# Gate and up of 20 FFN tiles as seven half-products in the place of eight

## The chip, the cores and the metric

The kernel runs on one core of one Trainium2 chip. The metric is the device time of one execution in microseconds (us); lower is better. The clock of TensorE (PE) was granted in full in every stretch of the profile.

## What is computed

One decoder layer of 1056 tokens (1024 of a prompt, 32 of eight short sequences) and 1024 features, all in fp32. The change touches the second FFN only:

```python
def swiglu_ffn(x, w_gate, w_up, w_down):
    return (jax.nn.silu(x @ w_gate) * (x @ w_up)) @ w_down
...
x = x + 0.5 * swiglu_ffn(rms_norm(x, ffn1[0]), ffn1[1], ffn1[2], ffn1[3])
y, h_last, new_conv, new_k, new_v = token_mixer(rms_norm(x, mix[0]), pos, h0, conv_buf, ...)
x = x + y
x = x + 0.5 * swiglu_ffn(rms_norm(x, ffn2[0]), ffn2[1], ffn2[2], ffn2[3])
```

`w_gate` and `w_up` are 1024 x 2816, `w_down` is 2816 x 1024.

## The kernel before

Features lie on the 128 partitions and tokens on the columns. The tokens are two halves: g=0 with 512 columns, g=1 with 544, which is two chunks of 272 (`CB`). The second half runs behind the first, and its FFN2 (`ffn(3, 1, ...)`) is the last piece of the program, with nothing beside it.

Every fp32 matrix product is three passes with the narrower type fp32r. Weights and activations are split into a high part (`whi`, `xh`) and the rest (`wlo`, `xl`), and PE adds whi.xh + whi.xl + wlo.xh (`mm3`, `mm3w`, lines 380 to 392). In g=1 each pass is two matmuls of 272 columns, one for each chunk, into two PSUM banks.

Weights come in units of 128 x 1024 fp32 (512 KB). SP loads a unit into one of two `raw` buffers, ACT writes `whi` (line 359), DVE writes `wlo` (line 361); three slots (`wslots`) hold split units. A gate or an up unit of an FFN tile f (128 of the 2816 columns) is 8 k-blocks x 3 passes x 2 chunks = 48 matmuls in g=1. So an ordinary tile of g=1 (`gu`) is 96 matmuls. A down unit is 48 as well. There are 22 tiles and 22 down units in g=1; down units stand in groups (two behind tile 3, then four behind tiles 6, 10, 14 and 18, four at the end).

In a tile of g=1 ACT takes silu of the gate out of PSUM (line 529), DVE multiplies it with the up product from PSUM (line 543), ACT and DVE split the result into `ha` for the down matmuls (lines 547, 549), and DVE adds each down product to x (`evd`, line 556). `prenorm` (lines 488 to 506) makes xh and xl for a stage; for the last stage it runs while PE works on the last down units of g=0.

No order is written by hand. The program is built by a planner in Python (`Sched`): each step is a generator that asks for an engine with a planned duration (`Req`), and the step that can start first is emitted next. The engines then run their queues in order, and wait on semaphores. A planned duration decides only the order.

Of the kernel before, what the change touches and what calls it, by code (L numbers as in the profile page):

```python
# [206 lines left out]
def layer(ctx: ExitStack, tc, t):  # L208
# [8 lines left out]
    NBIG, NPF, NH, NRM, NRAW, NW, NMX, NLW = 23, 3, 5, 6, 2, 3, 4, 1  # L217
# [33 lines left out]
    big, pff, hs, rms, banks = Pool(range(16, NBIG)), Pool(range(NBIG, NBIG + NPF)), Pool(range(NH)), Pool(range(NRM)), Banks()  # L251
# [88 lines left out]

    def loader():
        for n in range(2 * FIRST, len(order)):
            tk = yield Req("Q", 0.6, raws.soon(), when=raws.has(), lat=4.0)
            raw_of[n] = raws.get()[0]
            load_piece(n, 0)
            done(("raw", n, 0), tk)

    def splitter():
        for ns in [range(FIRST)] + [[n] for n in range(FIRST, len(order))]:
            for i, s in enumerate(pieces_of(ns[0])):  # L350
# [45 lines left out]
    def group(n, j, g, srcs, deps):  # L396
# [114 lines left out]
    def ffn(st, g, st2, u0, mode, rslot=None):
# [48 lines left out]
        def gu(f):  # L560
# [15 lines left out]
            if f == NF - 1:  # L576
                xfree(st2, g)

        xv = {m: ("x", st, g, m) for m in range(KD)}

        def down(gi, m0, mp):
            grp = GROUPS[gi]
            n = unit()
# [32 lines left out]
        for fn, k in steps:  # L616
# [784 lines left out]
    for g in range(2):  # L1401
# [3 lines left out]
        sc.spawn(prenorm(3, "g2", g), 2)  # L1405
# [133 lines left out]
```

## Time and profile before

| | |
|---|---|
| time, median of 3 runs | 1860.28 us (1860.11 to 1860.49) |
| the profiled execution: its own time | 1858.6 us |
| its span, first to last instruction | 1856.5 us |
| PE busy | 1850.5 us (100%), 11634 matmuls |
| DVE busy | 1064.3 us (57%) |
| ACT busy | 790.4 us (43%) |
| POOL busy | 12.3 us (1%) |
| DMA | 187.97 MB, mean 101 GB/s |

A matmul's own duration in the profile is longer than its step to the next one, since matmuls are pipelined; the distance between two starts is what one costs.

### The profile page before, as it was taken

How to read it: one execution, taken by the hardware profiler on the slowest of the kernel's cores; microseconds unless marked ns; L12 is line 12 of the kernel's file. 1: busy time of each engine (PE TensorE's matmuls, PEld its weight loads, DVE VectorE, ACT ScalarE, POOL GpSimd, SP SyncE). 2: the span in 40 equal slices, each digit the busy share in tenths (PEclk: the TensorE clock that was granted, in tenths of full speed). 3: DMA queues.
4: the chain of work that ended last, by engine and by line, in shares of the span. 5: the costliest groups of instructions: out<-in, count | busy, mean ns of one | idle time of the engine just before them, and what ended most of it. 6: DMA issues, size and time to landing. Idle time of an engine off the chain costs nothing.

```text
span 1856.5 us, 27927 instructions
## 1 busy us (share of the span) xinstructions
PE 1850.5 (100%) x11634; PEld 1691.5 (91%) x11634; DVE 1064.3 (57%) x1638; ACT 790.4 (43%) x1176; POOL 12.3 (1%) x39
## 2 busy tenths in 40 slices
PE   9999999999999999999999999999999999999999
PEld 7888888899999999999988988888898999999999
DVE  6774444466665777546576676865654543233333
ACT  6442222344746476424356566654533322222221
POOL 0000000000000000000000000000000000000000
PEclk9999999999999999999999999999999999999999
DMA  5432323242222322322242322232332422222222
GB/s 172 142 102 92 102 91 124 91 148 94 93 97 82 94 69 88 126 91 91 92 156 89 116 91 82 82 98 96 115 115 91 136 84 88 91 87 86 91 91 83
DMA packets 60253, 187.97 MB, mean 101 GB/s; under 512 B 7376, under 2 KB 9936, under 8 KB 60112
## 3 DMA queue, kind: packets, MB, share of 16 engines
q1 hardware_dynamic: 59984, 186.09, 30.3%
q8 instruction: 91, 1.49, 0.3%
q14 instruction: 34, 0.28, 0.0%
q10 hardware_dynamic: 144, 0.10, 0.0%
HBM read 174.58 MB, written 9.90 MB: 99 GB/s over the span
## 4 chain that ended last, share of the span: by engine, by line
PE 99%; DVE 0%; DMA 0%; ACT 0%; SPq 0%; issue 0%; ACTq 0%
PE ps L391 25%; PE ps L392 25%; PE ps L381 15%; PE ps L382 15%; PE ps L383 15%; PE ps L1060 1%; PE ps L795 0%; PE ps L1023 0%; PE ps L1022 0%; PE ps L1079 0%; PE ps L1078 0%; PE ps L911 0%; PE ps L317 0%; DMA fa<-x 0%; PE ps L1186 0%; DVE fa L556 0%
## 5 line engine op out<-in xcount | busy, mean ns | idle before, releaser
L359 ACT ACTIVATE whi<-raw 128x1024 fp32r<-128x1024 f32 (+1 forms) x312 | 325.3, 1043 | 686.7 <-issue 249.1
L361 DVE TENSOR_TENSOR wlo<-raw,whi 128x1024 fp32r<-128x1024 f32 (+1 forms) x312 | 375.4, 1203 | 194.0 <-ACT whi L359 188.1
L381 PE MATMUL ps<-xh,whi 128*128 128x512 f32 x880 | 345.2, 392 | 0.4 <-ACT xh L474 0.4
L383 PE MATMUL ps<-xh,wlo 128*128 128x512 f32 x880 | 342.9, 390 | 0.0
L382 PE MATMUL ps<-xl,whi 128*128 128x512 f32 x880 | 342.8, 390 | 0.1
L391 PE MATMUL ps<-xl,whi 128*128 128x272 f32 x880 | 254.4, 289 | 0.0
L392 PE MATMUL ps<-xh,wlo 128*128 128x272 f32 x880 | 254.2, 289 | 0.0
L391 PE MATMUL ps<-xh,whi 128*128 128x272 f32 x880 | 254.1, 289 | 0.0
L392 PE MATMUL ps<-xh,whi 128*128 128x272 f32 x880 | 253.5, 288 | 0.0
L391 PE MATMUL ps<-xh,wlo 128*128 128x272 f32 x880 | 253.4, 288 | 0.0
L392 PE MATMUL ps<-xl,whi 128*128 128x272 f32 x880 | 251.9, 286 | 0.0
L556 DVE SCALAR_TENSOR_TENSOR fa<-ps,fa 128x512 f32<-128x512 f32 (+1 forms) x192 | 135.6, 707 | 167.8 <-PE ps L392 100.7
L383 PEld LDWEIGHTS ps<-xh,wlo 128*128 128x128 f32 x880 | 165.2, 188 | 35.0
L381 PEld LDWEIGHTS ps<-xh,whi 128*128 128x128 f32 x880 | 165.4, 188 | 33.8 <-ACT xh L474 1.1
L382 PEld LDWEIGHTS ps<-xl,whi 128*128 128x128 f32 x880 | 165.3, 188 | 33.0 <-DVE xl L476 0.5
L391 PE MATMUL ps<-ha,whi 128*128 128x272 f32 x704 | 190.3, 289 | 0.0
L392 PE MATMUL ps<-ha,whi 128*128 128x272 f32 x704 | 189.8, 287 | 0.0
L391 PEld LDWEIGHTS ps<-xh,whi 128*128 128x128 f32 x880 | 165.8, 188 | 1.6
L392 PEld LDWEIGHTS ps<-xh,whi 128*128 128x128 f32 x880 | 165.4, 188 | 1.5
L391 PEld LDWEIGHTS ps<-xh,wlo 128*128 128x128 f32 x880 | 166.3, 189 | 0.0
L392 PEld LDWEIGHTS ps<-xh,wlo 128*128 128x128 f32 x880 | 166.0, 189 | 0.0
L392 PEld LDWEIGHTS ps<-xl,whi 128*128 128x128 f32 x880 | 165.9, 189 | 0.0
(238 smaller groups left out, 2723.0 us busy)
## 6 DMA issues: line engine op xcount, KB each, us to landing
raw<-w SPq DMA_DIRECT2D x304, 512.0 KB, 3.3
fa<-x SPq DMA_DIRECT2D x8, 272.0 KB, 3.8
xs<-fa SPq DMA_DIRECT2D x8, 272.0 KB, 4.9
fa<-xs SPq DMA_DIRECT2D x8, 272.0 KB, 2.9
y<-fa SPq DMA_DIRECT2D x8, 272.0 KB, 2.0
fa<-x SPq DMA_DIRECT2D x8, 256.0 KB, 4.4
xs<-fa SPq DMA_DIRECT2D x8, 256.0 KB, 4.2
fa<-xs SPq DMA_DIRECT2D x8, 256.0 KB, 3.4
```

Source lines behind the costliest of these rows:

```text
L359: S.activation(hi, raw, AF.Copy)
L361: V.tensor_tensor(lo, raw, f32(hi), OP.subtract)
L381: PE.matmul(p, wh, ah, start=first, stop=False)
L382: PE.matmul(p, wh, al, start=False, stop=False)
L383: PE.matmul(p, wl, ah, start=False, stop=last)
L391: PE.matmul(ps[:, b, :CB], w, a[:, c0], start=s, stop=e)
L392: PE.matmul(ps[:, b + 1, :CB], w, a[:, c1], start=s, stop=e)
L556: V.scalar_tensor_tensor(x, P_(b, g), fac, x, op0=OP.mult, op1=OP.add)
L1060: PE.transpose(ps[:, bk, j * 128:(j + 1) * 128], P[j // 2][:, j % 2, hf * 128:(hf + 1) * 128], ident)
```

## The change

In g=1 the gate and up products of tiles 2 to 21 are computed by Strassen's scheme in Winograd's form. Let x1 and x2 be features 0 to 511 and 512 to 1023, a and b the two chunks, G1, G2, U1, U2 the halves (512 rows) of the tile's gate and up weights. The eight half-products of a tile become seven, each 4 k-blocks x 3 passes = 12 matmuls of 272 columns, on sums of weights and sums of activations:

- weights: s1 = U1+U2, s2 = s1-G1, s3 = G2-s2, s4 = G1-U1, four POOL additions of 128 x 512 for every tile (`sums`);
- activations: T1 = x1b-x1a, T2 = x2b-T1, T3 = x2b-x1b, T4 = x2a-T2, 16 POOL subtractions of 128 x 272 once (`xsums`), then split by ACT and DVE (`small`); T1 to T3 go where xh and xl of g=0 were, T4 over x1b once the two ordinary tiles are through;
- products in PE's order: P1 = x1a.G1, P5 = T1.s1, P6 = T2.s2, P3 = x2b.s3, P7 = T3.s4, P2 = x2a.G2, P4 = T4.U2.

P1, P6, P7 and P4 are added up in one bank. ACT copies this bank into SBUF behind P1, P6 and P7 (`copy_of`), and the next of them waits for the copy. P5 and P3 share a second bank, copied behind P5; P2 has a third. `ev7` makes the tile's result out of the three banks and the four copies.

Gate and up weights of such a tile are loaded as four pieces of 128 x 512 into general buffers (`fa`) and split as seven pieces of 128 x 512, two in a slot. Three more `fa` buffers and a fourth one for tile results are added; the buffers of x of g=0 are given back when its output is stored. The first two of the last four down units run abreast.

```diff
-    NBIG, NPF, NH, NRM, NRAW, NW, NMX, NLW = 23, 3, 5, 6, 2, 3, 4, 1
+    NBIG, NPF, NH, NRM, NRAW, NW, NMX, NLW = 26, 4, 5, 6, 2, 3, 4, 1
...
     def loader():
-        for n in range(2 * FIRST, len(order)):
+        n = 2 * FIRST - 1
+        while n + 1 < len(order):
+            n += 1
+            if n in pairs:
+                tk = yield Req("Q", 1.0, tok["xt",], big.soon(4), when=lambda: big.n() >= (4 if summing[0] else 8) and waiting[0] < 2, lat=4.0)
+                waiting[0] += 1
+                raw_of[n] = [big.get()[0] for _ in range(4)]
+                for i, r in enumerate(raw_of[n]):
+                    SP.dma_start(F(r, 0), t["w"][order[n + i // 2], :, i % 2 * 512:i % 2 * 512 + 512])
+                done(("raw", n, 0), tk)
+                n += 1
+                continue
...
+    def sums(n, ss):
+
+        g1, g2, u1, u2 = (F(i, 0) for i in raw_of[n])
+        a, b, c, d = (F(i, 0) for i in ss)
+        for i, (o, x, y, op) in enumerate(((a, u1, u2, OP.add), (b, a, g1, OP.subtract), (c, g2, b, OP.subtract), (d, g1, u1, OP.subtract))):
+            tk = yield Req("G", 1.3, tok["raw", n, 0])
+            G.tensor_tensor(o, x, y, op)
+            done(("sum", n, i), tk)
...
+    def split_pair(n):
+
+        yield Req("G", 0.0, tok["raw", n, 0], big.soon(4), when=big.has(4))
+        ss = [big.get()[0] for _ in range(4)]
+        summing[0] += 1
+        sc.spawn(sums(n, ss), 1)
+        g1, g2, u1, u2 = raw_of[n]
+        wplace[n] = []
+        for i, (src, dep) in enumerate(((g1, 0), (ss[0], 1), (ss[1], 1), (ss[2], 1), (ss[3], 1), (g2, 0), (u2, 0))):
+            dep = tok[("sum", n, i - 1) if dep else ("raw", n, 0)]
+            if i % 2 == 0:
+                tk = yield Req("A", 0.55, dep, wslots.soon(), when=wslots.has())
+                wplace[n].append(wslots.get()[0])
+            else:
+                tk = yield Req("A", 0.55, dep)
+            c = slice(i % 2 * 512, i % 2 * 512 + 512)
+            hi, lo = whi_t[:, wplace[n][-1], c], wlo_t[:, wplace[n][-1], c]
+            S.activation(hi, F(src, 0), AF.Copy)
+            tk = yield Req("D", 0.6, tk)
+            V.tensor_tensor(lo, F(src, 0), f32(hi), OP.subtract)
+            done(("w", n, i), tk)
+        waiting[0] -= 1
+        summing[0] -= 1
+        big.put(Tok(max(tk.t, tok["sum", n, 3].t)), *raw_of[n], *ss)
+
...
-                               when=lambda: banks.has(1 + g)() and main_out[0] + g < MAINCAP)
+                               when=lambda: banks.has(1 + g)() and main_out[0] + g < (8 if tok['plain', 3, 1].t else MAINCAP))
...
+    def xsums(ys, k, tk):
+        (y1a, y1b), (y2a, y2b) = ((ys[m][:, :CB], ys[m][:, CB:]) for m in (k, k + 4))
+
+        for o, x, y in ((y1a, y1b, y1a), (y1b, y2b, y1b), (y2b, y2b, y1a), (y2a, y2a, y2b)):
+            tk = yield Req("G", 0.85, tk)
+            G.tensor_tensor(o, x, y, OP.subtract)
+        done(("xsum", k), tk)
...
+    def prenorm_pairs(st, name, g):
...
+        big.put(Tok(0.0), *range(NBIG - 3, NBIG))
+        yield Req("A", 0.0, big.soon(9), when=big.has(9))
+        tmp = [big.get()[0] for _ in range(9)]
+        out, *ys = (F(i, g) for i in tmp)
+        done(("xt",), Tok(0.0))
...
+        for m in range(KD + 1):
+            if m < KD:
+                tk = yield Req("D", dD(g))
+                V.scalar_tensor_tensor(ys[m], xap(m, g), col(name, m), out, op0=OP.mult, op1=OP.mult)
+                tkn = yield Req("A", dA(g), tk)
+                S.activation(xh[g][:, m], ys[m], AF.Copy)
+            if m:
+                m -= 1
+                tkd = yield Req("D", dD(g), tka)
+                V.tensor_tensor(xl[g][:, m], ys[m], f32(xh[g][:, m]), OP.subtract)
+                done(("xs", st, g, m), tkd)
+            tka = tkn
+            if m >= 4:
+                sc.spawn(xsums(ys, m - 4, tkd), 1)
+        big.put(tkd, tmp[0])
...
+        for i in range(4):
+            if i == 3:
+                yield Req("A", 0.0, tok["plain", st, g])
+            for k in range(4):
+                (y1a, y1b), (y2a, y2b) = ((ys[m][:, :CB], ys[m][:, CB:]) for m in (k, k + 4))
+                yield from small((y1a, y2b, y1b, y2a)[i], i, k, tok["xsum", k])
+                if i > 1:
+                    big.put(tok["xt", i, k], tmp[1 + k + 4 * (i == 3)])
...
+        def copy_of(b, to, tk, name, f):
+            tk = yield Req("A", 0.33, tk)
+            S.activation(to, ps[:, b, :CB], AF.Copy)
+            done((name, f), tk)
...
+        def ev7(f, bs, a, c):
...
+            tk = yield Req("D", dh, tok["P3", f], tok["mV", f])
+            V.tensor_tensor(a[:, z1], q, a[:, z1], OP.add)
...
+            tk = yield Req("D", dh, tok["P2", f])
+            V.tensor_tensor(a[:, z0], p, a[:, z0], OP.add)
...
+            tks = yield Req("A", dA(g), tk, sets=(S_SET,))
+            S.activation(a, a, AF.Silu)
+            yield Req("D", dh, tok["mW", f])
+            V.tensor_tensor(c[:, z1], c[:, z0], c[:, z1], OP.add)
+            yield Req("D", dh, tks)
+            V.tensor_tensor(c[:, z1], c[:, z1], a[:, z1], OP.mult)
...
+            tk = yield Req("D", dh, tok["P4", f])
+            V.tensor_tensor(c[:, z0], v, a[:, z0], OP.mult)
...
+            hh, hl = (ha[:, H[f], i, :TW[g]] for i in range(2))
+            tk = yield Req("A", dA(g), tk)
+            S.activation(hh, c, AF.Copy)
+            tk = yield Req("D", dD(g), tk)
+            V.tensor_tensor(hl, c, f32(hh), OP.subtract)
...
+        def gu7(f):
+
...
+            yield Req("P", 0.0, pff.soon(2), when=pff.has(2))
+            a, c = (pff.get()[0] for _ in range(2))
...
+            plan7 = (("P1", 0, x1a, "", ("m1", F(a, g)[:, z0])), ("P5", 1, t1, "", ("m5", F(c, g)[:, z1])), ("P6", 0, t2, "m1", ("mV", F(a, g)[:, z1])),
+                     ("P3", 1, x2b, "m5", None), ("P7", 0, t3, "mV", ("mW", F(c, g)[:, z0])), ("P2", 2, x2a, "", None), ("P4", 0, t4, "mW", None))
+            for i, (name, b, xs, after, then) in enumerate(plan7):
+                deps = [tok["w", n, i]] + [d for _, d in xs]
+                dur = 12 * CB / 2400 * 1.01
+                if after:
+                    tk = yield Req("P", dur, *deps, tok[after, f])
+                elif b == len(bs):
+                    tk = yield Req("P", dur, *deps, banks.soon(), when=lambda: banks.has()() and main_out[0] < 8)
+                    bs.append(banks.get())
+                    main_out[0] += 1
+                w = wplace[n][i // 2]
+                for k, ((h, l), _) in enumerate(xs):
+                    o = i % 2 * 512 + k * 128
+                    wh, wl = whi_t[:, w, o:o + 128], wlo_t[:, w, o:o + 128]
+                    for j, (x, y) in enumerate(((wh, h), (wh, l), (wl, h))):
+                        PE.matmul(ps[:, bs[b], :CB], x, y, start=not after and k == j == 0, stop=k == 3 and j == 2, skip_group_check=bool(after))
+                if i % 2 or i == 6:
+                    wslots.put(tk, w)
+                done((name, f), tk)
+                if then:
+                    sc.spawn(copy_of(bs[b], then[1], tk, then[0], f), 0)
+                if i == 5:
+                    sc.spawn(ev7(f, bs, a, c), 0)
...
+            if gi == len(GROUPS) - 1 and plain < NF:
+                return [(lambda: down(gi, 0, mp, 2), 2, False)] + [(lambda m0=m0: down(gi, m0, mp), 1, False) for m0 in range(2 * mp, KD, mp)]
...
+    plan += ffn(3, 1, 4, U_FFN2, "silu", plain=2)
...
+            tk = yield Req("Q", 0.6, tok["x", 4, g, m], lat=4.0)
             SP.dma_start(t["y"][:, m, T0[g]:T0[g] + TW[g]], xap(m, g))
+            if g == 0:
+                big.put(tk, X[g][m])
...
-        sc.spawn(prenorm(3, "g2", g), 2)
+        sc.spawn((prenorm_pairs if g else prenorm)(3, "g2", g), 2)
```

Where it shows, as the built programs list it. First PE: the start of an ordinary unit (before), and the end of P6 with the start of P3 (now). `xh_66` and `xl_68` are the splits of g=0, in which T1 to T3 now lie, `xh_67` and `xl_69` those of g=1. Before:

```order
L392 MATMUL ps<-xh_67,wlo 128x272
L391 MATMUL ps<-xh_67,whi 128x272 [waits Activation_49]
L392 MATMUL ps<-xh_67,whi 128x272
L391 MATMUL ps<-xl_69,whi 128x272
L392 MATMUL ps<-xl_69,whi 128x272
L391 MATMUL ps<-xh_67,wlo 128x272 [waits DVE_49]
L392 MATMUL ps<-xh_67,wlo 128x272
```

Now:

```order
L775 MATMUL ps<-xh_66,wlo 128x272
L775 MATMUL ps<-xh_66,whi 128x272
L775 MATMUL ps<-xl_68,whi 128x272
L775 MATMUL ps<-xh_66,wlo 128x272
L775 MATMUL ps<-xh_67,whi 128x272 [waits Activation_49]
L775 MATMUL ps<-xl_69,whi 128x272
L775 MATMUL ps<-xh_67,wlo 128x272 [waits DVE_49]
L775 MATMUL ps<-xh_67,whi 128x272
```

Where both chunks followed each other on one set of weights in two banks, a half-product now adds twelve matmuls to one bank. The waits on ACT and DVE, which stood every 48 matmuls, stand every 12; here P3 waits for the copy behind P5.

Second ACT, in a run of tiles without down units between them. Before, from one silu to the next (L359 is the split of a weight unit, L529 silu, L547 the split of a tile's result):

```order
L529 ACTIVATE fa<-ps 128x544 [waits PE_49]
L359 ACTIVATE whi<-raw 128x1024 [waits DMAHW1_49,Activation_49]
L359 ACTIVATE whi<-raw 128x1024 [waits DMAHW2_49,PE_49,Activation_49]
L547 ACTIVATE ha<-fa 128x544 [waits DVE_49]
L529 ACTIVATE fa<-ps 128x544 [waits PE_49]
```

Now, from behind one silu to the next (L728; L401 splits a weight piece, L708 is a copy out of PSUM, L739 the split of a tile's result):

```order
L401 ACTIVATE whi<-fa 128x512 [waits PE_49,Activation_49,Pool_49] x2
L739 ACTIVATE ha<-fa 128x544 [waits DVE_49]
L708 ACTIVATE fa<-ps 128x272 [waits PE_49]
L401 ACTIVATE whi<-fa 128x512 [waits DMAHW3_49]
L708 ACTIVATE fa<-ps 128x272 [waits PE_49]
L401 ACTIVATE whi<-fa 128x512 [waits DMAHW5_49,Activation_49]
L708 ACTIVATE fa<-ps 128x272 [waits PE_49]
L401 ACTIVATE whi<-fa 128x512 [waits DMAHW6_49,Activation_49]
L401 ACTIVATE whi<-fa 128x512 [waits DVE_49,PE_49,Pool_49]
L708 ACTIVATE fa<-ps 128x272 [waits PE_49]
L401 ACTIVATE whi<-fa 128x512 [waits DVE_49,Pool_49]
L728 ACTIVATE fa<-fa 128x544 [waits DVE_49]
```

Four instructions for a tile became thirteen, seven splits of half the width and four copies among them. No copy has more than two other instructions between it and the copy ahead of it, except across silu.

Third DVE, at the change from g=0 to g=1. Before (L556 adds a down product of g=0, L502 normalises a block of x, L504 writes `xl` of one block, L361 `wlo`):

```order
L504 TENSOR_TENSOR xl_69<-fa,xh_67 128x544 [waits Activation_49]
L556 SCALAR_TENSOR_TENSOR fa<-ps,fa 128x512 [waits PE_49]
L502 SCALAR_TENSOR_TENSOR fa<-fa,cols 128x544 [waits DVE_49]
L361 TENSOR_TENSOR wlo<-raw,whi 128x1024 [waits DMAHW2_49,Activation_49]
L504 TENSOR_TENSOR xl_69<-fa,xh_67 128x544
L504 TENSOR_TENSOR xl_69<-fa,xh_67 128x544 [waits Activation_49]
L361 TENSOR_TENSOR wlo<-raw,whi 128x1024 [waits DMAHW5_49,PE_49,Activation_49]
```

Now (L681, L602, L608 and L427 are the same lines in the changed file, L621 splits T1):

```order
L602 SCALAR_TENSOR_TENSOR fa<-fa,cols 128x544
L681 SCALAR_TENSOR_TENSOR fa<-ps,fa 128x512 [waits PE_49]
L608 TENSOR_TENSOR xl_69<-fa,xh_67 128x544 [waits Activation_49]
L427 TENSOR_TENSOR wlo<-raw,whi 128x1024 [waits DMAHW2_49,Activation_49]
L602 SCALAR_TENSOR_TENSOR fa<-fa,cols 128x544
L608 TENSOR_TENSOR xl_69<-fa,xh_67 128x544 [waits Activation_49] x2
L621 TENSOR_TENSOR xl_68<-fa,xh_66 128x272 [waits Activation_49]
L427 TENSOR_TENSOR wlo<-raw,whi 128x1024 [waits DMAHW5_49,PE_49,Activation_49]
```

The last normalisation of x (L502, now L602) stood ahead of the split of a weight unit and stands behind it now; the splits of the sums follow at once.

## Rows read from the trace of the kernel before

**Rows 1.** The page: its first line, and its chain of work that ended last, by engine.
```profile
span 1856.5 us, 27927 instructions
PE 99%; DVE 0%; DMA 0%; ACT 0%; SPq 0%; issue 0%; ACTq 0%
```

**Rows 2.** Waits of PE, whole span: line, releaser, us in total, times, longest.
```profile
PE ps L652 <- DVE rm L650: 1.6, 1, 1.6
PE ps L381 <- ACT xh L474: 0.4, 1, 0.4
```

**Rows 3.** Busy time by stretch, from the first rows of the second half on.
```profile
core 0: us, PE busy (x) PEld busy (x) DVE busy (x) ACT busy (x) POOL busy (x), PEclk, DMA share, GB/s
1600.00:1700.00 100.00, 100.00 (x800) 100.00 (x799) 36.87 (x40) 24.88 (x30) 0.00 (x0) 1.00 0.26 87
```

**Rows 4.** PE in order of time: last 512-column matmuls, first and last 272-column ones.
```profile
1439.77 0.39 PE L383 MATMUL ps<-ha,wlo 128*128 128x512 f32 x1
1455.17 0.39 PE L383 MATMUL ps<-ha,wlo 128*128 128x512 f32 x1
1455.40 0.29 PE L391 MATMUL ps<-xh,whi 128*128 128x272 f32 x1
...
1852.44 0.29 PE L392 MATMUL ps<-ha,wlo 128*128 128x272 f32 x1
```

**Rows 5.** Tile ps from 1455 us: the down matmuls, with first and last start.
```profile
L391 PE MATMUL ps<-ha,whi x352: 287/289/290, 1503.5 to 1852.1; 128*128 128x272 f32 x176
```

**Rows 6.** Order of time: last matmul of a gate unit, and ACT behind it.
```profile
1473.31 0.29 PE L392 MATMUL ps<-xh,wlo 128*128 128x272 f32 x1
1473.64 0.62 ACT L529 ACTIVATE fa<-ps 128x544 f32<-128x544 f32 x1 [4.53 <-PE ps L392]
```

**Rows 7.** Groups of ACT and DVE by shape, 1455 to 1855 us.
```profile
L359 ACT ACTIVATE whi<-raw 128x1024 fp32r<-128x1024 f32 x64 | 67.7, 1058 | 186.3 <-PE ps L392 106.7 <-issue 79.6
L547 ACT ACTIVATE ha<-fa 128x544 fp32r<-128x544 f32 x22 | 14.4, 657 | 0.0
...
L361 DVE TENSOR_TENSOR wlo<-raw,whi 128x1024 fp32r<-128x1024 f32 x64 | 78.4, 1226 | 115.0 <-ACT whi L359 113.5
L549 DVE TENSOR_TENSOR ha<-fa,ha 128x544 fp32r<-128x544 f32 x22 | 15.8, 719 | 0.0
```

**Rows 8.** Groups of ACT and DVE by shape: the nearest to 272 and 512 columns.
```profile
L288 ACT ACTIVATE rm<-ps 128x256 fp32r<-128x256 f32 x6 | 2.3, 384 | 11.0 <-PE ps L1186 11.0
...
L547 ACT ACTIVATE ha<-fa 128x512 fp32r<-128x512 f32 x2 | 1.2, 617 | 0.0
...
L1209 DVE TENSOR_TENSOR rm<-ps,rm 128x256 fp32r<-128x256 f32 x8 | 3.4, 422 | 6.9 <-ACT rm L288 6.9
...
L549 DVE TENSOR_TENSOR ha<-fa,ha 128x512 fp32r<-128x512 f32 x2 | 1.4, 684 | 0.0
```

**Rows 9.** All of POOL by shape: four of its groups.
```profile
L738 POOL COPY stc<-fa 128x24 f32<-128x24 f32 x4 | 1.9, 472 | 0.0
L737 POOL COPY stc<-fa 128x3 f32<-128x3 f32 x4 | 0.7, 187 | 395.9 <-ACT fa L288 395.9
L1118 POOL MEMSET rm<- 128x512 f32 x1 | 0.5, 530 | 37.2 <-PE ps L1078 37.2
...
L1528 POOL MEMSET const-float32-1.0<- 128x1 f32 x1 | 0.1, 103 | 0.0
```

**Rows 10.** DVE in order of time, where the second half's FFN2 begins.
```profile
1455.60 0.69 DVE L556 SCALAR_TENSOR_TENSOR fa<-ps,fa 128x512 f32<-128x512 f32 x1
1456.20 0.78 DVE L502 SCALAR_TENSOR_TENSOR fa<-fa,cols 128x544 f32<-128x544 f32 x1
1456.90 1.22 DVE L361 TENSOR_TENSOR wlo<-raw,whi 128x1024 fp32r<-128x1024 f32 x1
1458.03 1.36 DVE L504 TENSOR_TENSOR xl<-fa,xh 128x544 fp32r<-128x544 f32 x2
```

**Rows 11.** DMA issues: KB each, median us to landing.
```profile
fa<-w SPq DMA_DIRECT2D x4, 256.0 KB, 4.6
```

More of the change, by code (lines that the diff above doesn't have):

```diff
@@ L508, in xfree, with ffn @@
     def xfree(st, g):
         done(("xfree", st, g), Tok(sc.free["P"] + 0.15))
[L511 removed]
+    def ffn(st, g, st2, u0, mode, rslot=None, plain=NF):
         H, spart = {}, {}
@@ new lines, in gu7 @@
+        def gu7(f):
+            while hs.n() < 1:
+                yield Req("P", 0.0, when=hs.has())
+            H[f] = hs.get()[0]
+            n = unit()
+            unit()
+            yield Req("P", 0.0, pff.soon(2), when=pff.has(2))
+            a, c = (pff.get()[0] for _ in range(2))
+            bs = []
+            z0, z1 = slice(0, CB), slice(CB, 2 * CB)
+            x1a, x2a, x2b = ([((xh[g][:, m, z], xl[g][:, m, z]), tok["xs", st, g, m]) for m in ms] for ms, z in ((range(4), z0), (range(4, 8), z0), (range(4, 8), z1)))
+            t1, t2, t3, t4 = ([(xt(i, k), tok["xt", i, k]) for k in range(4)] for i in range(4))
+            plan7 = (("P1", 0, x1a, "", ("m1", F(a, g)[:, z0])), ("P5", 1, t1, "", ("m5", F(c, g)[:, z1])), ("P6", 0, t2, "m1", ("mV", F(a, g)[:, z1])),
[22 more added lines that the diff above has]
+                    sc.spawn(ev7(f, bs, a, c), 0)
+            if f == NF - 1:
+                xfree(st2, g)
@@ L579, in ffn, with down @@
         xv = {m: ("x", st, g, m) for m in range(KD)}
-        def down(gi, m0, mp):
+        def down(gi, m0, mp, nu=1):
             grp = GROUPS[gi]
-            n = unit()
+            ns = [unit() for _ in range(nu)]
             srcs = [tuple(ha[:, H[f], i, :TW[g]] for i in range(2)) for f in grp]
@@ L592, in down @@
             if gi == len(GROUPS) - 1 and m0 == 0:
-                for j, (b, tk) in enumerate((yield from abreast([group(n, j, g, srcs, deps) for j in range(mp)]))):
+                for j, (b, tk) in enumerate((yield from abreast([group(ns[j // mp], j % mp, g, srcs, deps) for j in range(nu * mp)]))):
                     end(j, b, tk)
@@ L597, in down @@
                 for j in range(mp):
-                    b, tk = yield from group(n, j, g, srcs, deps)
+                    b, tk = yield from group(ns[0], j, g, srcs, deps)
                     end(j, b, tk)
-            wrelease(n, tk)
-            if m0 + mp == KD:
+            for n in ns:
+                wrelease(n, tk)
+            if m0 + mp * nu == KD:
                 for f in grp:
@@ L615, in ffn @@
         out = []
-        for fn, k in steps:
+        for fn, k, seven in steps:
+            fn.seven = seven
             out.append((fn, list(range(u, u + k))))
@@ L1368, in layer @@
     plan += merge(ffn(3, 0, 4, U_FFN2, MODES[2]), mixer(1))
-    plan += ffn(3, 1, 4, U_FFN2, "silu")
-    for _, us in plan:
+    plan += ffn(3, 1, 4, U_FFN2, "silu", plain=2)
+    for fn, us in plan:
+        if getattr(fn, "seven", False):
+            pairs.add(len(order))
         order += us
```

45 lines of the change are left out of this document (41 added, 4 removed).

## The prediction, made before the run

> **What bounds the kernel now.** I read the page first: the chain that ended last is 99% PE [rows 1], and PE's waits add up to 2.0 us, all before the first product [rows 2]. So nothing but PE's own stream sets the end, and a change pays by taking matmuls out of that stream and loses by making PE wait. Then the stretch that is changed. By PE's timeline, the last 512-column matmul of g=0 starts at 1455.17, the first one of the second half's FFN2 at 1455.40 and the last at 1852.44 [rows 4]; the stage is 397 us and 3168 matmuls (44 gate and up units and 22 down units of 48). The windows show what the other engines have left there: in 100 us PE holds 800 matmuls at the full granted clock, DVE is busy for 37 us, ACT for 25, POOL never [rows 3]. At the end one down product is evicted and stored behind the last matmul; that stays as it is.
>
> **Removed from PE.** 20 tiles fall from 96 to 84 matmuls: 240 in all, and the built program has just 240 fewer. One costs the distance between two starts. The first eight gate and up units are 384 matmuls, from 1455.40 to the first down matmul at 1503.5 [rows 4, 5]: 48.1 / 384 = 0.1253 us, and 800 in 100 us is 0.125 [rows 3]. 240 x 0.1253 = **30.1 us** saved. Ahead of 1455 us nothing moves on PE: the built orders are alike up to the second tile's end, so the fourth result buffer costs and brings nothing there.
>
> **The new stream's pace.** Twelve matmuls in a row now add to one bank, where two banks took turns. The half with 512 columns already adds to one bank: 66 steps between 1439.77 and 1455.17 [rows 4], 0.2333 us for 512 columns or 0.456 ns a column, against 0.1253 / 272 = 0.461. So one bank is no slower, and I cost it at nothing. A half-product then takes 12 x 0.1253 = 1.50 us, a tile 10.5, a down unit 6.0.
>
> **Four waits for copies in each tile.** Each copied product has one half-product (1.50 us) as cover before PE needs its bank again. ACT starts 0.33 us after the last matmul's start [rows 6], which is 0.20 after its 0.125. The copy of 272 columns from PSUM is not there; 256 columns take 0.384 us, 512 columns of SBUF 0.617 and 544 columns 0.657 [rows 7, 8], so some 0.40. The way back to PE I take as long as the way out, 0.20. Together 0.80 of 1.50; spare 0.70. What can stand ahead of a copy on ACT is one instruction already running, at most 0.66 us. Two short splits stand ahead of the fourth copy in ACT's queue, but the copy before them is two half-products (3.0 us) older, since P3 lies between. So the copies cost **0**; the cover that hides them is P5, P6, P3 and P2, and were it gone, each 0.1 us on 80 copies would be 8 us.
>
> **Load of ACT and DVE.** For a tile ACT gets 7 x 0.62 + 4 x 0.40 + 2 x 0.66 = 7.3 us, DVE 7 x 0.68 + 5 x 0.42 + 0.72 = 7.6 us [rows 7, 8], of 10.5; a down unit adds 1.06 and 1.23 us for its split and two 0.7 us evictions to 6.0 us. Neither becomes the bound. The three slots now cover less: a slot holds two half-products (3.0 us of PE) where it held 6.0. The planner frees a slot when its second half-product is through, so a piece can be split from 4.5 us ahead of its use. The work on it is 0.62 + 0.68 + 0.3 for two semaphores = 1.6 us; lead 2.9 us. Cost 0 while DVE is not held up by more than that.
>
> **POOL's additions.** No two-input POOL instruction of any size is in the trace. From below: DVE takes 0.684 us for two inputs of 512 columns [rows 8]. From above: POOL's copies take 0.187 us for 3 columns and 0.472 for 24 [rows 9], 13.6 ns a column, so 7.1 us for 512; these copies read short strided pieces. The nearest in shape is the memset of 512 columns, 0.530 us, of which 0.103 is the fixed part of a one-column memset [rows 9]. It moves one stream; an addition moves three: 3 x 0.43 + 0.10 = 1.4 us, and 0.8 for 272 columns. I take these: 5.6 us of POOL for a tile of 10.5 us, hidden, since the pieces of a tile are loaded about a tile ahead (a load of 256 KB lands in 4.6 us [rows 11]).
>
> **The change from g=0 to g=1.** This is the one place with little room. Before, the last `xl` ends at 1458.03 + 1.36 = 1459.4 [rows 10]; PE reads the last k-block's `xl` as its 45th matmul, at 1455.40 + 44 x 0.1253 = 1460.9. Now the last normalisation stands behind the weight split: eviction to 1456.2, an `xl` to 1456.9, the split to 1458.1, normalisation to 1458.8, ACT's part 0.66, last `xl` to 1460.2. Margin 0.7 us. From 1455 on POOL also runs the 16 subtractions. If they hold DVE up by one of them (0.8 us) at each of its four last instructions with two SBUF inputs, that is 3.2 - 0.7 = 2.5 us of PE; if not, 0. I take half, **1.25 us**. The sums themselves end at 1455 + 16 x 0.8 = 1468 and their twelve splits, 0.4 us each on either engine, some 6 us later; the first P5 needs them at 1455.4 + 24 + 1.5 = 1481.
>
> **Waits that are met.** PE passes some 15 semaphores in a tile instead of four. The 0.125 us of the windows [rows 3] holds the boundaries of some 16 units with their waits, so a met wait shows no price there; at most 0.01 us each, 20 x 11 x 0.01 = 2.2 us. I take 0.5.
>
> **Sum.** 1856.5 - 30.1 + 1.25 + 0.5 = 1828.2 span; the profiled execution lies 2.1 us above its span (1858.6), so 1830.3; the median of the runs is 1.7 above that execution, so **1832 us**.
>
> **Weighed against the skill.** The rows show DVE's instructions with two SBUF inputs, the splits, at 0.68 and 1.23 us with POOL idle [rows 7 to 9]; nothing here shows both at once. The Trainium skill, "SBUF — State Buffer", section Who interferes with whom, says that a DVE instruction with two SBUF inputs and a POOL instruction that reads SBUF exclude each other: the second to issue waits for the first to end. By it the seven splits and both engines' time add up, which is the first rival. The skill's "GPSIMD Engine Reference", section 3.1, gives 4497 ns for a two-input addition of 2048 columns, an estimate of 1.1 us for 512; by that the four additions take 4.4 us of a tile and rival 1 loses 8 - 17, that is nothing.
>
> **Rivals.** 1. *DVE and POOL shut each other out.* In a tile DVE's two-input work from SBUF is, with starts packed as closely as the trace shows (1.13 us from split to next at 1456.90 [rows 10], 0.60 for half), 7 x 0.60 + 0.63 + 2 x 0.33 = 5.5 us; from PSUM 3 x 0.33 = 1.0; POOL 5.6. Sum 12.1 against 10.5: 1.6 us too much in each of 20 tiles, less the lead of 2.9 us once for each of six runs of tiles between down units: 32 - 17 = 15 us lost, **1847**. For it: POOL works half of each tile, just where DVE is busy. Against it: the order leaves DVE idle for 3 us of a tile, where additions fit.
> 2. *Copies late.* If ACT is held ahead of a copy by an instruction that itself waits (a split waits for POOL or a slot), the 0.70 us of spare go. At 0.2 us late on each of 80 copies, 16 us are lost: **1848**; at 0.38 all is lost.
> 3. *POOL becomes the bound, slower than before.* With the down units a tile has 10.5 + 22 x 6.0 / 20 = 17.1 us, so four additions are hidden up to 4.3 us each; from (397 - 24) / 80 = 4.7 us on the kernel is slower than before. At the upper bound of 7.1 it would take 1860 + 80 x 7.1 - 373 = **2055**. Against it: contiguous rows, and a memset at 0.53.
> 4. *One bank costs.* 1680 matmuls of 272 columns now follow each other on one bank; 18 ns each would eat the gain, **1860**. The 512-column stream speaks against it.
>
> **How the numbers follow.** Forecast 0.70; rival 1 0.15, rival 2 0.08, rival 3 0.04, rival 4 0.03. The low end is no stall anywhere, 1830.2, less 0.7; the high end takes in the most at the change (2.5), met waits at 2.2 and most of rivals 1 and 2: 1846. Left out is rival 3, the worst of 1 and 2 and half of 4, under 0.2. A measurement of this kernel tells 0.2% (3.7 us) from no change. Faster: the forecast, rival 1, most of rival 2, 0.93; same 0.02 (rivals 2 and 4); slower 0.05 (rival 3, a little of 2 and 4).
>
> **What would show it.** 2928 matmuls from 1455.4 to about 1824, at 0.125 us from start to start inside a half-product. No wait of PE for ACT's copies; a short one for DVE's `xl` at 1460. Copies of about 0.4 us that start 0.2 us behind their product. POOL's addition at 1.0 to 1.5 us. I am wrong if POOL's addition takes over 4 us, if DVE's half-width split is far above 0.68 us while POOL runs and PE waits for `wlo`, or if PE's step inside a half-product is above 0.13.

## The result, and the profile after

The changed kernel takes **1841.18 us** (median of 4 runs, 1840.33 to 1842.38) against 1860.31 for the kernel before on the same chip: a ratio of 0.9903, 95% interval 0.9891 to 0.9915. That is 19.1 us less, inside the predicted range, but 9 us above the predicted 1832. The profiled execution has a span of 1838.5 us against 1856.5 [rows 1]. In the experiments below, one execution of the kernel with additions in halves ran at a granted clock of 0.57 and took 2943 us, and is left out of that kernel's median.

First the page of the changed kernel: its first line and its chain of work that ended last.

```profile
span 1838.5 us, 28166 instructions
...
PE 18%; DVE 2%; issue 1%; DMA 0%; ACT 0%; DVEq 0%
```

Before, the chain was PE from end to end [rows 1]; now its shares cover the last fifth of the span and cross DVE, so PE waits. The waits of PE over the whole span say for what (line, releaser, us in total, times, longest), as in [rows 2]:

```profile
PE ps L775 <- DVE fa L734: 5.9, 4, 2.8
PE ps L864 <- DVE rm L862: 1.6, 1, 1.6
PE ps L457 <- DVE xl L608: 1.6, 2, 1.4
PE ps L775 <- DVE xl L621: 1.6, 1, 1.6
```

Only the second was there before. The order of time gives each its full gap between two matmul starts: 1.68 + 0.47 at 1459 to 1462 (`xl`, the change from g=0 to g=1), 1.85 at 1490.87 (`xl` of T4), 3.08 at 1494.45, and 1.34, 1.33 and 1.33 at 1598.48, 1666.11 and 1733.73 (these four for L734, the last eviction of a tile). Together 11.1 us, of which 0.9 is the matmuls' own distance. Then the windows (busy us and instructions of PE, weight loads, DVE, ACT, POOL, granted clock, DMA share, GB/s):

```profile
1480.00:1500.00 20.00, 15.65 (x116) 15.21 (x115) 17.61 (x22) 9.20 (x19) 11.50 (x8) 0.95 0.57 197
1500.00:1550.00 50.00, 50.00 (x394) 50.00 (x394) 34.64 (x52) 24.94 (x46) 11.76 (x9) 0.98 0.11 38
1600.00:1700.00 100.00, 98.96 (x787) 98.74 (x788) 66.70 (x96) 47.04 (x84) 26.22 (x19) 1.00 0.31 106
```

Behind the two gaps at 1491 to 1497 the granted clock falls below 1.00; between 1498.16 and 1501.54 the matmuls start 0.227 us apart, which is the lower clock level (1.2 GHz), and that costs another 1.5 us. From 1600 to 1700 PE does 787 matmuls where it did 800, and DVE is busy for 67 us where it was 37 [rows 3]. The stage, from the first 272-column matmul at 1454.50 to the last at 1834.48, takes 379.98 us against 397.04 [rows 4]: 17.1 saved of 30.1, 13.0 given back: 10.2 in gaps, 1.5 at the lower clock, 1.3 in steps too small to show as a wait (half of it the first step behind each gap, 0.23 us for 0.125).

Why DVE is late, stands in the groups by line (busy us, mean ns of one | idle before, releasers), 1455 to 1835, beside [rows 7, 8]:

```profile
L403 DVE TENSOR_TENSOR wlo<-fa,whi 128x512 fp32r<-128x512 f32 x140 | 128.8, 937 | 22.3 <-ACT whi L401 20.4
...
L725 DVE TENSOR_TENSOR fa<-ps,fa 128x272 f32<-128x272 f32 x20 | 8.8, 439 | 16.1 <-PE ps L775 16.1
...
L381 POOL TENSOR_TENSOR fa<-fa 128x512 f32<-128x512 f32 x80 | 115.5, 1457 | 204.3 <-DMA fa<-w 92.3 <-DVE wlo L403 76.4 <-DVE wlo L427 29.3
...
L708 ACT ACTIVATE fa<-ps 128x272 f32<-128x272 f32 x80 | 31.8, 398 | 53.3 <-PE ps L775 52.8
```

The copies (398 ns) and the evictions from PSUM (439) are what the forecast took. The half-width split `wlo` is not: 937 ns on average where 684 was expected [rows 8]. Single instructions part into two sorts. The 95 `wlo` of the stage that run while POOL is idle take 0.684 us; the 45 that overlap an instruction of POOL take 1.47 on average and up to 1.80. The evictions from PSUM take 0.43 us in either case. One place, engine by engine in order of time (start, us, engine, line; the last bracket is idle time and its releaser):

```profile
1650.74 1.29 POOL L381 TENSOR_TENSOR fa<-fa 128x512 f32<-128x512 f32 x1 [0.68 <-POOL fa L381]
1658.28 7.86 POOL L381 TENSOR_TENSOR fa<-fa 128x512 f32<-128x512 f32 x5 [6.25 <-DVE wlo L403]
...
1663.81 1.18 DVE L730 TENSOR_TENSOR fa<-fa 128x272 f32<-128x272 f32 x1
1664.91 1.78 DVE L403 TENSOR_TENSOR wlo<-fa,whi 128x512 fp32r<-128x512 f32 x1
1666.61 0.43 DVE L732 TENSOR_TENSOR fa<-fa 128x272 f32<-128x272 f32 x1
1666.96 0.43 DVE L734 TENSOR_TENSOR fa<-ps,fa 128x272 f32<-128x272 f32 x1
...
1664.61 0.29 PE L775 MATMUL ps<-xh,wlo 128*128 128x272 f32 x1
...
1666.11 0.29 PE L775 MATMUL ps<-xh,wlo 128*128 128x272 f32 x1
1667.44 0.40 PE L775 MATMUL ps<-xh,whi 128*128 128x272 f32 x1 [1.04 <-DVE fa L734]
...
1667.42 0.66 ACT L739 ACTIVATE ha<-fa 128x544 fp32r<-128x544 f32 x1 [1.80 <-DVE fa L734]
1667.99 0.38 ACT L708 ACTIVATE fa<-ps 128x272 f32<-128x272 f32 x1
```

An addition that meets no such instruction of DVE takes POOL 1.29 us. Through the five at 1658.28, POOL and DVE take turns: L730 needs 1.18 us instead of 0.43, `wlo` 1.78 instead of 0.685. So L734, which itself reads PSUM and takes its usual 0.43 us, ends late: 2.78 us after P4's last matmul starts (1664.61), where the kernel without additions, the first experiment below, has 0.92. It frees the PSUM bank of P4, and the planner has given just that bank to P5 of the next tile. P1 lies between and ends with the matmul at 1666.11, so P5 would start at 1666.24, 1.63 us after P4's last matmul: the bank has some 0.7 us to spare, L734 is 1.9 us late, and PE's first matmul of P5 stands at 1667.44. (`Banks._pick` prefers a free bank whose neighbour is in use, which is the one just freed.) ACT is held as well: `hh` (L739) waits for L734, and the next tile's first copy stands behind `hh`.

### The profile page after: what moved, and what is told of

It is laid out like the page before. It is cut to its first block, busy times and chain, and to the rows that moved or that the text cites. A ratio compares the mean times of both kernels' runs of the same rounds, so it can differ in the third digit from the quotient of the medians.

```text
span 1838.5 us, 28166 instructions
## 1 busy us (share of the span) xinstructions
PE 1823.7 (99%) x11394; PEld 1663.7 (90%) x11394; DVE 1179.6 (64%) x1834; ACT 865.0 (47%) x1372; POOL 144.8 (8%) x135
## 5 line engine op out<-in xcount | busy, mean ns | idle before, releaser
L425 ACT ACTIVATE whi<-raw 128x1024 fp32r<-128x1024 f32 (+1 forms) x272 | 282.9, 1040 | 532.9 <-PE ps L448 207.9
L427 DVE TENSOR_TENSOR wlo<-raw,whi 128x1024 fp32r<-128x1024 f32 (+1 forms) x272 | 327.2, 1203 | 83.7 <-ACT whi L425 79.1
L681 DVE SCALAR_TENSOR_TENSOR fa<-ps,fa 128x512 f32<-128x512 f32 (+1 forms) x192 | 135.6, 707 | 157.4 <-PE ps L458 90.2
L449 PEld LDWEIGHTS ps<-xh,wlo 128*128 128x128 f32 x880 | 165.2, 188 | 35.1
L447 PEld LDWEIGHTS ps<-xh,whi 128*128 128x128 f32 x880 | 165.3, 188 | 33.5 <-ACT xh L540 0.8
L448 PEld LDWEIGHTS ps<-xl,whi 128*128 128x128 f32 x880 | 165.3, 188 | 33.2 <-DVE xl L542 0.8
L775 PE MATMUL ps<-xh,whi 128*128 128x272 f32 x560 | 162.0, 289 | 5.9 <-DVE fa L734 5.9
L775 PE MATMUL ps<-xl,whi 128*128 128x272 f32 x560 | 162.3, 290 | 1.6 <-DVE xl L621 1.6
L457 PE MATMUL ps<-xl,whi 128*128 128x272 f32 x560 | 162.0, 289 | 1.6 <-DVE xl L608 1.6
L775 PE MATMUL ps<-xh,wlo 128*128 128x272 f32 x560 | 162.7, 291 | 0.0
L457 PE MATMUL ps<-xh,whi 128*128 128x272 f32 x560 | 162.1, 289 | 0.0
L458 PE MATMUL ps<-xh,wlo 128*128 128x272 f32 x560 | 161.7, 289 | 0.0
L458 PE MATMUL ps<-xh,whi 128*128 128x272 f32 x560 | 161.4, 288 | 0.0
L457 PE MATMUL ps<-xh,wlo 128*128 128x272 f32 x560 | 161.3, 288 | 0.0
L458 PE MATMUL ps<-xl,whi 128*128 128x272 f32 x560 | 160.4, 286 | 0.0
L403 DVE TENSOR_TENSOR wlo<-fa,whi 128x512 fp32r<-128x512 f32 x140 | 128.8, 937 | 22.3 <-ACT whi L401 20.4
L448 PE MATMUL ps<-ha,whi 128*128 128x512 f32 x352 | 138.9, 395 | 0.0
```

The costliest lines, as they stand in the source:

```text
L403: V.tensor_tensor(lo, F(src, 0), f32(hi), OP.subtract)
L425: S.activation(hi, raw, AF.Copy)
L427: V.tensor_tensor(lo, raw, f32(hi), OP.subtract)
L447: PE.matmul(p, wh, ah, start=first, stop=False)
L448: PE.matmul(p, wh, al, start=False, stop=False)
L449: PE.matmul(p, wl, ah, start=False, stop=last)
```

## The experiments

The theory (A): a POOL instruction that reads SBUF and a DVE instruction with two SBUF inputs exclude each other, so POOL's additions are paid in DVE's time, and PE loses where something that DVE releases has little lead: a bank (A1). The rivals: the order of the new work alone makes DVE late (B), POOL's being busy or its sums' lateness (C), the late copies of the prediction's rival 2. All ratios below are to the kernel before, on the same chip. Over these chips the kernel before took 1858.3 to 1860.5 us, so where two changed kernels lie within 2 us of each other, their stages in the traces are compared.

**No additions.** The line of the weight addition is left out, and the four splits read raw pieces.

```diff
-            G.tensor_tensor(o, x, y, op)
...
-        for i, (src, dep) in enumerate(((g1, 0), (ss[0], 1), (ss[1], 1), (ss[2], 1), (ss[3], 1), (g2, 0), (u2, 0))):
+        for i, (src, dep) in enumerate(((g1, 0), (u1, 1), (g1, 1), (g2, 1), (u1, 1), (g2, 0), (u2, 0))):
```

> Left out: POOL's 80 weight additions; the splits of the four sums read raw pieces instead, so the output is not the reference's. The 16 subtractions of x stay. Theory A (a POOL instruction that reads two SBUF inputs holds up DVE instructions with two SBUF inputs, and the late DVE eviction behind them keeps the bank that P5 of the next tile wants): the full-width wlo split is back at 0.69 us everywhere in the stage, the four waits of PE for the last eviction (3.1 + 3 x 1.3 us), the wait for T4 (at most 1.8 us) and the stretch at the lower clock (1.5 us) go, the 2.1 us at the change of g stay: about 1831 us. Rival B (the order of the new work alone makes DVE late, whatever POOL does): the same four waits, about 1841 us.

Measured: 1830.32 us, 0.9843 (0.9827 to 0.9859). `wlo` takes 0.688 us on average; the only waits left in the stage are the 2.2 us of gaps at 1459 to 1462, where POOL's subtractions of x still run. The last matmul of a P4, and the eviction behind it (L733, L734 above), as they stand in this kernel:

```profile
1657.34 0.29 PE L774 MATMUL ps<-xh,wlo 128*128 128x272 f32 x1
...
1657.83 0.43 DVE L733 TENSOR_TENSOR fa<-ps,fa 128x272 f32<-128x272 f32 x1
```

DVE, ACT and PE run the same instructions in the same order as in the changed kernel (and do so with memsets, with doubled and with halved additions below), and DVE is not late: L733 ends 0.92 us after that matmul starts. Rival B falls.

**Memsets for additions.** The same instants, as much POOL time, no reading.

```diff
-            G.tensor_tensor(o, x, y, op)
+            for _ in range(3):
+                G.memset(o, 0.0)
```

> Left out: the values of the weight sums. Each of the 80 additions is replaced by three memsets of its output, 3 x 0.53 = 1.6 us of POOL, which waits for the same data and releases the same splits but reads nothing from SBUF; the output is not the reference's. Theory A (what holds up DVE is that POOL reads SBUF while DVE wants two SBUF inputs): the wlo split stays at 0.69 us beside a busy POOL, and the time is that of the kernel without additions, about 1831 us. Rival C (POOL being busy at all, or the sums coming late to the splits): POOL is as busy as with additions, so the waits stay, about 1841 us.

Measured: 1830.16 us, 0.9841 (0.9826 to 0.9855). The groups of DVE and of POOL in the stage:

```profile
L404 DVE TENSOR_TENSOR wlo<-fa,whi 128x512 fp32r<-128x512 f32 x140 | 94.1, 687 | 29.9 <-ACT whi L402 27.1
...
L382 POOL MEMSET fa<- 128x512 f32 x240 | 123.1, 526 | 186.4 <-DVE wlo L404 169.7 <-issue 7.5
```

POOL is busy for 123 us, more than with the additions (115.5), and `wlo` stays at 687 ns: the 68 of them that overlap an instruction of POOL take 0.690 us. It is the reading that shuts DVE out, not POOL's being busy, and not the wait for the sums, which the memsets pass on just as late. Rival C falls. No run has a POOL instruction that reads one input only.

**Twice as many additions.** Each addition is issued twice.

```diff
             G.tensor_tensor(o, x, y, op)
+            G.tensor_tensor(o, x, y, op)
```

> Nothing left out; each of the 80 additions on POOL is done twice. Theory A (POOL's reading time is added to DVE's in the same stretch): DVE is held up by up to twice as much, more tiles have a wait for the last eviction than four, the loss over the kernel without additions (11 us) at least doubles: 1852 to 1870 us. Rival B (the four waits come from the order of the work): 1841 us, as long as POOL's 160 additions end in time.

Measured: 1872.19 us, 1.0073 (1.0058 to 1.0088), slower than before the change. `wlo` rises to 1248 ns, and the waits grow at the same place first (waits of PE):

```profile
PE ps L776 <- DVE fa L735: 24.8, 11, 4.5
PE ps L776 <- ACT fa L709: 2.3, 1, 2.3
```

(L735 is L734, one line lower.) The loss over the kernel without additions goes from 11 to 42 us, more than in proportion, and 2 us beyond the top of what theory A expected: what the first additions use up is lead.

**Copies twice.** Each of the 80 copies from PSUM is issued a second time.

```diff
             S.activation(to, ps[:, b, :CB], AF.Copy)
+            S.activation(to, ps[:, b, :CB], AF.Copy)
```

> Nothing left out; each of the 80 copies from PSUM to SBUF on ACT is done twice (0.40 us more each). Forecast (a copy has 0.70 us of spare before PE wants its bank): 0.30 is left, so 1841 us, up to 2 us more where ACT is late already. Rival 2 of the prediction (copies are late when ACT is held up): each of the tiles with a late ACT loses up to 0.4 us at several copies, 1845 to 1860 us.

Measured: 1842.99 us, 0.9914 (0.9899 to 0.9928). PE waits for no copy in the stage; the three waits for L734 near 1600, 1668 and 1736 rise from 1.33 to 1.76 us, by the 0.4 us of one copy, and so does the wait for T4 (1.85 to 2.27): that is the 1.7 us by which the stage is longer. So a copy has at least 0.40 us to spare ahead of PE, and rival 2 has no direct part in the 11 us. But a copy stands on ACT ahead of the `whi` (1657.69 in the changed kernel) with which the late chain of DVE begins, so a longer copy makes L734 later.

**Another bank for P5.** The seven-product unit takes the bank that has been free for longest.

```diff
+    def oldest(self):
+        b = min((t.t, i) for i, t in self.free.items())[1]
+        del self.free[b]
+        return b
...
-                    bs.append(banks.get())
+                    bs.append(banks.oldest())
```

> Nothing left out. The seven-product unit takes the bank that has been free for longest instead of the one that the planner prefers. Theory A1 (the late DVE costs PE time only because P5 takes the bank that the last eviction of the tile before has just given back): the four waits for that eviction go, with the stretch at the lower clock 3.1 + 3 x 1.3 + 1.5 = 8.5 us, DVE's instructions as long as they were: about 1833 us. Rival D (the next thing that hangs on DVE, wlo or hl, is just as late): PE waits there instead, 1839 to 1841 us.

Measured: 1836.44 us, 0.9873 (0.9859 to 0.9888): 4.7 us less than the changed kernel, of some 8 expected. `wlo` is as slow as ever (937 ns), the waits for L734 and the lower clock are gone (clock 1.000), but a new wait stands in their place:

```profile
PE ps L780 <- ACT fa L713: 2.3, 4, 0.8
PE ps L462 <- DVE xl L613: 1.6, 2, 1.4
PE ps L780 <- DVE xl L626: 1.6, 1, 1.6
```

(L713 is the copy, L708 before.) P6 wants the bank of P1, whose copy stands behind `hh`, and `hh` behind the late L734. So A1 and its rival D each hold for a part: the bank was what DVE's lateness reached first, and the copy behind `hh` comes next, not `wlo` or `hl`, which D named. An ACT instruction that itself waits and holds a copy up behind it is what the prediction's rival 2 describes; the wait for the bank had hidden it.

**Subtractions of x later.** Their place in the planner's list is moved behind the last `xl`.

```diff
-            if m >= 4:
-                sc.spawn(xsums(ys, m - 4, tkd), 1)
+        for k in range(4):
+            sc.spawn(xsums(ys, k, tkd), 1)
```

> Nothing left out. POOL's 16 subtractions of x start behind the last xl of g=1 instead of beside the last four. Theory A (the four last normalisation and xl instructions are held up by these subtractions): xl L608 back at 0.72 us, the 2.1 us of waits at 1459 to 1462 go, about 1839 us, if the splits of T1 to T4, now some 3 us later, still come before their products; the wait for T4 (1.8 us) may grow by up to 3 us. Rival (the change of g is late for the order of DVE alone): no change there, 1841 us or later.

Measured: 1841.23 us, 0.9899 (0.9884 to 0.9914), no change. The edit did not do what it was for. POOL has nothing ahead of the subtractions in its queue, and they wait for their own rows of x alone, so it starts them at once:

```profile
1453.70 2.27 POOL L586 TENSOR_TENSOR fa<-fa 128x272 f32<-128x272 f32 x2 [3.88 <-DVE fa L602]
```

The gaps at 1459 to 1462 shrink from 2.2 to 1.4 us, and the waits at T1 to T4 move about with no gain; the wait of 2.8 us for L734 behind them becomes one of 2.8 us for `wlo`. So the time, which is that of the rival in the expectation, says nothing for it.

**Additions on DVE, and subtractions too.** First the 80 additions alone, then with the 16 subtractions, these behind the last `xl` (the lines moved as above).

```diff
-            tk = yield Req("G", 1.3, tok["raw", n, 0])
-            G.tensor_tensor(o, x, y, op)
+            tk = yield Req("D", 0.69, tok["raw", n, 0])
+            V.tensor_tensor(o, x, y, op)
...
-            tk = yield Req("G", 0.85, tk)
-            G.tensor_tensor(o, x, y, OP.subtract)
+            tk = yield Req("D", 0.43, tk)
+            V.tensor_tensor(o, x, y, OP.subtract)
```

> Nothing left out. The 80 weight additions move from POOL to DVE (about 0.69 us each, as the split of the same shape); the 16 subtractions of x stay on POOL. Theory A (additions on POOL cost DVE their own length while they shut it out, and come between DVE's instructions in an order that the planner doesn't know): DVE pays 80 x 0.69 = 55 us of 380, in its queue where the planner puts them; the four waits for the last eviction and the stretch at the lower clock go, the 2.1 us at the change of g stay: 1830 to 1833 us. Rival (it is the amount of DVE's work between two down units that is too much, wherever the additions stand): waits of the same size or longer, 1840 us or more.

> Nothing left out. As the kernel with the additions on DVE, and the 16 subtractions of x on DVE too, behind the last xl (putting them later on POOL's list alone did not help: POOL took them at 1453.7 us all the same, since they wait only for the normalisation). Theory A: xl L608 takes 0.72 us again, so the 2.1 us at 1459 to 1462 go as well: 2 us under the kernel with the additions alone on DVE, 1828 to 1831 us. Rival (the change of g is late for DVE's own work, 16 subtractions more in it): no gain there, or a wait for T1 or T4, 1 to 4 us above it.

Measured: 1849.75 us, 0.9949 (0.9934 to 0.9964), and 1844.31 us, 0.992 (0.9903 to 0.9937). The first expectation is wrong by 17 us and the second by 13; the time that came out is that of the first's rival (too much work for DVE, 1840 us or more). `wlo` is back at 687 ns, an addition costs DVE 0.71 us, yet PE waits more. The waits of PE in the first of the two, and behind them its chain of work in order of time (start, us, what) at one of them:

```profile
PE ps L775 <- ACT whi L401: 5.4, 8, 1.1
PE ps L775 <- DVE xl L621: 3.3, 1, 3.3
PE ps L775 <- DVE wlo L403: 2.0, 9, 0.3
```

```profile
1602.98 0.04 ACT fa L708
...
1603.27 0.63 ACT whi L401
...
1603.92 0.70 DVE wlo L403
...
1604.67 1.40 PE ps L775 x9
```

But DVE is not full there, as that rival would have it: busy for 10.9 of the 15 us from 1590 to 1605. The split `whi` of the next piece stands on ACT behind the copy of the running product, and can start only when that product is through. My reading is that the planner, with the sums as late as DVE gave them, queued the copy first; no run tested it. The second kernel has the same waits for `whi` (5.1 us), but those at 1459 to 1462 are gone, as expected, and its clock is 1.000 (0.998 in the first).

**Bank and subtractions together; the planner told.** The first kernel has the bank's edit and the subtractions on DVE, the additions stay on POOL. The second has, besides, 0.75 us of DVE booked for each addition.

```diff
-            G.tensor_tensor(o, x, y, op)
+            G.tensor_tensor(o, x, y, op); sc.free["D"] = max(sc.free["D"], tk.t - 1.45) + 0.75
```

> Nothing left out. Two edits together: the bank that has been free for longest (1836.4 us alone), and the 16 subtractions of x on DVE behind the last xl; the weight additions stay on POOL. Theory A: the 2.1 us at 1459 to 1462 go, as they did with all additions on DVE, and the wait for T4 (1.8 us) shrinks to the 1.2 us seen there: 1833 to 1834.5 us. Rival: DVE's 7 us of subtractions push the splits and the bank waits of the first tiles later, no gain: 1836 us or more.

> Nothing left out. As the kernel with both edits, and the planner books 0.75 us of DVE for each weight addition on POOL, so that its order reckons with the exclusion. Theory A (part of what is left comes from an order made for a faster DVE: hh and the next copy stand in the wrong order on ACT): the waits for the copy m1 (0.5 to 0.8 us, four of them) go, 1830.5 to 1833 us. Rival (the order cannot help, since the additions' real times are set by the data and the semaphores): within 1 us of the kernel with both edits.

Measured: 1834.25 us, 0.987 (0.9855 to 0.9885), and 1839.3 us, 0.9895 (0.9878 to 0.9911), 5 us worse. The first time is as expected, but not all of the way there: the gaps at 1459 to 1462 and the wait for T4 are gone, and PE waits 2.6 us for `wlo` at 1489 to 1497 instead. Booking did remove the wait for the copy, but the new order makes PE wait four times for `wlo` (5.3 us in all, up to 1.5). Theory and rival both missed this: here an order made with a mean price for the exclusion is worse than one made without.

**Additions in halves.** From the changed kernel, two instructions of 256 columns for each one of 512.

```diff
-            G.tensor_tensor(o, x, y, op)
+            for h in range(2):
+                G.tensor_tensor(o[:, h * 256:h * 256 + 256], x[:, h * 256:h * 256 + 256], y[:, h * 256:h * 256 + 256], op)
```

> Nothing left out; from the changed kernel, each of the 80 weight additions is cut into two of 256 columns. Theory A1 (what hurts is the length of a single hold-up, the 0.75 us or more that one DVE instruction waits for the POOL instruction ahead): wlo beside POOL falls from 1.42 to about 1.05 us and the four waits shrink by half, 1837 to 1839 us. Theory A2 (what hurts is the sum of both engines' times in the stretch, which the cut does not change, and the fixed part of 80 more instructions adds to): wlo ends as late as before, 1841 to 1845 us.

Measured: 1836.24 us, 0.988 (0.9863 to 0.9896); the stage is 4.7 us shorter than in the changed kernel. POOL needs more time, and DVE less:

```profile
L404 DVE TENSOR_TENSOR wlo<-fa,whi 128x512 fp32r<-128x512 f32 x140 | 112.4, 819 | 22.7 <-ACT whi L402 21.1
...
L382 POOL TENSOR_TENSOR fa<-fa 128x256 f32<-128x256 f32 x160 | 139.3, 908 | 176.0 <-DMA fa<-w 111.2 <-DVE wlo L404 64.8
```

One of 256 columns takes 0.74 us alone, so two take 1.48 against 1.29. But `wlo` beside POOL falls from 1.47 to 1.01 us, the waits for L734 from 5.9 to 2.9 us, and the wait for T4 is gone. What hurts is how long DVE is kept waiting, not the sum of both engines' times, which rose. Whether it is the length of a single hold-up or their total, this run does not part: the total for `wlo` fell too, from 35 to 18 us (140 x 0.13).

**All three.** Bank, subtractions on DVE, additions in halves.

> Nothing left out. Three edits together: the bank that has been free for longest, the subtractions of x on DVE, the weight additions on POOL in halves of 256 columns. Theory A1 (three separate places of one cause): the waits for the copy m1 (0.8 us, three of them), which remained behind the bank edit, shrink with DVE's lateness of about 0.5 us less, and those for wlo at 1489 to 1497 (2.6 us) in part: 1831 to 1833 us, close to the 1830.2 us of the kernel with memsets for additions. Rival (the edits remove the same waits, so they don't add up): 1834 us, that of the two edits.

Measured: **1829.52 us** (5 runs, 1829.39 to 1830.02), 0.984 (0.9827 to 0.9853), level with the two kernels that leave the additions out, and 1.5 us below what was expected. The waits of PE:

```profile
PE ps L870 <- DVE rm L868: 1.6, 1, 1.6
PE ps L781 <- DVE wlo L409: 0.7, 3, 0.3
PE ps L454 <- DVE xl L548: 0.3, 1, 0.3
```

Of the 11 us of gaps, 1.6 are left; the waits for copies are gone altogether. The stage runs from 1455.01 to 1824.12, 369.1 us, 27.9 less than before; with no wait at all the forecast's 30.1 would be that less.

## Why the prediction was right, and where it was wrong

**Right, as sized.** 240 matmuls less at 0.1253 us: in the memset kernel and the last one the stage comes within 3 us of the whole 30.1. One bank costs nothing: 0.125 us from start to start. The copies: 398 ns for 0.40, 0.2 us behind their product, and no wait of PE for one, even doubled. Met waits: 0.5 was taken, and 1 us or so is left beside the gaps (in the last kernel 30.1 - 27.9 less 1.2 of gaps). POOL's addition alone: 1.29 us for the 1.4 taken.

**Wrong: the step that called POOL's 5.6 us for a tile "hidden"**, and with it "cost 0 while DVE is not held up by more than" 2.9 us. The additions are paid in DVE's time: `wlo` at 937 ns for 687 is 140 x 0.25 = 35 us more of DVE. Price for PE: the four waits for L734 (5.9), T4 (1.6) and the lower clock (1.5), 9.0 us. The lead of 2.9 us was worked out for `wlo`, and in the changed kernel it held: PE never waited for `wlo` there. It was not far off, though: with another order, in three of the kernels above, PE waited 2.6 to 5.3 us for `wlo`. The prediction's sign of being wrong was thus half met: the split was far above 0.68 us beside POOL, and PE waited for something else. What I did not ask is what else DVE releases, with less lead: the bank of the last eviction, which P5 takes 1.63 us behind P4 and which has 0.7 us to spare, and `hh`, behind which a copy waits.

**Rival 1 had the mechanism** (chance 0.15): 15 us worked out, 10.9 measured (1841.2 less the 1830.3 of the kernel without additions), and its 1847 lies nearer to the result than the forecast. That is luck in part: it spread the loss over every tile and set it against the lead of `wlo`, where PE lost at a few places and to another release. The rule weighed there, from the Trainium skill's "SBUF — State Buffer", section Who interferes with whom, is borne out by the memset kernel and the rows: 0.684 us alone, 1.47 beside a reading POOL, 0.690 beside a writing one, and no change for a DVE instruction with one input in PSUM. I gave it too small a chance because the order leaves DVE idle for 3 us of a tile; but POOL runs its additions in bursts of four or five, when the data come, and there DVE is full (busy for 9.85 of the 10 us from 1590 to 1600). The Trainium skill's "GPSIMD Engine Reference", section 3.1, led to an estimate of 1.1 us for 512 columns; measured alone it is 1.29.

**The change of g** cost 2.2 us of gaps, 1.9 beyond the matmuls' own distance, for 1.25 taken (bound 2.5): the subtractions hold up three `xl` (1.28 to 1.32 us for 0.72), a normalisation (1.29) and a split (1.79 for 1.23). With the subtractions on DVE behind them, the gaps are gone.

The time fell into the range only because the high end had been drawn to take in most of rivals 1 and 2; by the forecast's own step it is 9 us out, and by the span 10.3 (1838.5 for 1828.2), since from span to median it added 3.8 us where 2.7 were measured.

## What to carry to other kernels

Work given to an idle POOL is not free when it reads SBUF and DVE is splitting or adding from SBUF: price it as DVE time, cut it short (halves cost 15% more POOL time for an addition alone here and saved 4.7 us), and put it where DVE idles. When an engine becomes late, list everything that it releases, and ask of each what lead it has: the buffer just freed and taken again has the least (0.7 us here, where `wlo` had 2.9), and a planner that prefers it turns a hidden delay into a wait. An order that a planner makes is no knob with a sign: moving the additions to the engine that pays for them, and telling the planner of the price, both made it worse here.

## What the runs showed of the hardware

POOL's addition of two 512-column inputs takes 1.29 us alone and up to 1.77 in turns with DVE; of 256 columns 0.74, so by these two sizes the fixed part is about 0.19 us (0.74 - 0.55). A 512-column `wlo` that meets POOL takes up to 1.80 us, that is 1.1 longer, close to a whole addition; with additions of 256 columns up to 1.29 (the last kernel), 0.60 longer. A DVE instruction of 272 columns with one input in PSUM takes 0.43 to 0.44 us beside POOL or not. Two waits of PE of 1.85 and 3.08 us, 1.7 us apart, were followed by 3.4 us at the lower clock, and so was a single one of 2.4 us in the kernel with additions in halves (2.7 us); single waits of 1.3 us were not. The pair of 1.7 and 0.5 us at the change of g was followed by the lower clock in the kernel with additions on DVE (3.2 us) and not in the changed kernel.
